# A hybrid recurrent and attention block on one core: gt2's pieces and the DRAM sums placed later, gt2's loads on ScalarE's queue, x1 transposed under the output projection

## The chip, the cores and the metric

The kernel runs on one core of one Trainium2 chip. The metric is the time of one execution on the device in microseconds (us). It was 2109.33 us, the median of three runs (2107.52 to 2113.61). The engines are named as the profile names them: PE (matrix multiplication), PEld (its weight load), DVE (VectorE), ACT (ScalarE), POOL (GpSimd) and SP (the engine that issues most DMAs).

## The reference

One layer on 512 tokens of width 2048, all in 32-bit floats. Six modulation vectors (sh1, sc1, gt1, sh2, sc2, gt2, each of 2048) come from one product of the conditioning vector with a matrix of 2048 x 12288.

```
mod = silu(c) @ w_ada + b_ada;  sh1, sc1, gt1, sh2, sc2, gt2 = split(mod, 6)
h = rms_norm(x, g_mix) * (1 + sc1) + sh1
xr, yr, q, k, v, f_logit = split(h @ w_in)
y_rec = rglru_group(xr, yr, ...)                 # conv, gates, scan, gelu gate
y_att = forgetting_attention_group(q, k, v, f_logit, ...)
mix = concat(rms_norm(y_rec, g_out_rec), rms_norm(y_att, g_out_att))
x = x + gt1 * (mix @ w_out)                      # "x1" in the kernel
h2 = rms_norm(x, g_ffn) * (1 + sc2) + sh2
gate, up = split(h2 @ w_up)                      # width 5632 each
x = x + gt2 * ((silu(gate) * up) @ w_down)
```

## The kernel before, in words

Features lie on the 128 partitions and the 512 tokens along the free dimension, so the width of 2048 is 16 tiles of 128 x 512 (kt 0 to 15). Every product is done in three matmuls of a reduced 32-bit type: weights and activations are each split into a high part (a copy by ACT, line 226) and a low part (a difference by DVE, line 227), and high x high, high x low and low x high are summed in PSUM. So each block of weights passes through SP (load), ACT, DVE and PE. The weights' high and low parts have three buffers each (lines 224 and 225).

The stages of the stretch that matters here:

- The output projection, four groups wo0 to wo3 (line 852). A group makes four tiles of x1 out of 16 steps of 12 matmuls; the function `fm_group` (line 246) calls small functions ("hooks") after given steps. The tiles of a group are read out of PSUM by DVE right behind it; for wo0 to wo2 they are finished (gt1, plus x) by `x1_fin` (line 847) as hooks of the next group, at steps 5, 7, 9 and 11. `square_acc` (line 313) squares each finished tile on ACT and adds it on DVE to the tile ssq_1; `make_hr` (line 836) splits x1 for the up phase.
- The first two up groups, up0 and up1 (line 1000), done in the same way on the unnormalised x1. In up0, hooks at steps 7 and 9 (R1STEP) make r1, the reciprocal root of the mean square: `rstd_parts` (line 284) sums ssq_1 over the partitions with four matmuls, POOL takes the root, four more matmuls spread it over the partitions, and ACT copies it. Hooks at steps 2, 4, 6 and 8 (X_STEPS) run `x1_by_tokens` (line 897): PE transposes a quarter of x1, 16 tiles of 128 x 128 per block, ACT copies it out of PSUM and SP stores it to DRAM, where the end of the kernel reads it. From r1 on, `make_t` (line 913) makes eight sets of sums and differences of the normalised input for the fast phase.
- The fast up phase, f4 to f43 (line 1051). Each f makes its 128 columns with seven products of half size in place of eight; it loads two chunks of 1 MB of weights (`fast_chunk`, line 1020; the loads are line 1029), and makes further sums of blocks on DVE (lines 1038 to 1042).
- The down phases (line 1170), which read sums of weight blocks.

Two kinds of side work run along the up phase. The text places them by n, the number of the chunk (0 to 79):

- gt2: `gt2_piece` (line 174), 64 pieces. A piece is a load of 128 x 512 of the modulation matrix (256 KB, line 171, on SP's queue) and one multiplication on DVE that also sums along the row (line 181). Piece n issues the load of piece n + 1. Its tile has the tag "ssq" with two buffers, which it shares with ssq_x, ssq_att, ssq_rec and ssq_1. The text has piece n at chunk n.
- DRAM sums: `sums24` (line 972), for q from 0 to 10. A sum copies two blocks of 1 MB of the down weights from DRAM to DRAM (lines 975 and 976, on SP, tied behind the last weight load that the text has before it) and then adds three blocks by accumulating DMAs of POOL (line 970). The text begins sum q at chunk 3 + 6q.

The order on each engine's queue is not the order of the text: a planner in the tile framework lays the instructions out by priority (later in the text is lower, `tc.high_priority` raises it) as soon as it believes the inputs and the buffer to be there. Each engine then runs its own list strictly in that order. `ada_some` (line 197) works through the other modulation vectors in the same way, five blocks in each wo group.

Of the kernel before, what the change touches and what calls it, by code (L numbers as in the profile page):

```python
# [39 lines left out]
MIX_STEPS = (12, 13, 14, 15)  # L40
FORGET_STEP = 4
MIXREC_STEPS = (1, 4)
R1STEP = (7, 9)
T_STEPS = ((10, 11, 13, 15), (0, 4, 9, 15))
YR0_AHEAD = 80
CARRY = (0, 0, 1, 1, 1, 3, 3, 6)
# [5 lines left out]
HS = S // 2  # L52
NP = KT // 2
STD = 2
X_STEPS = (2, 4, 6, 8)
NQ = FT // 4


# [5 lines left out]
def block_kernel(ctx, tc, xT, crow, adaT, vecs, bfr, w1, wyr, wqkv0, wqkv, wgate, wout, wup0, wups, wdn, outT):  # L64
# [16 lines left out]
    def page(name, tag, shape=None):  # L81
        return pgp.tile(shape or [P, S], F32, tag=tag, name=name, bufs=TAGS[tag])

    def acc(name):
        return psa.tile([P, S], F32, tag="acc", name=name)
# [82 lines left out]

    def gt2_load(n):
        t = cp.tile([P, S], F32, name=f"gt2_{n}", tag="ssq", bufs=2)  # L170
        nc.sync.dma_start(out=t, in_=adaT[GT2 * KT + n // 4, :, (n % 4) * S:(n % 4 + 1) * S])
        gt2_src[n] = t

    def gt2_piece(n):
# [109 lines left out]
    def rstd_parts(ssq, n, name, inv=None, times=None, bank=None):  # L284

        tok = small(NT, name + "t")
        bank = bank or rgp

        def sums():
            ps = bank(name + "a")  # L290
            for t in range(NT):
                nc.tensor.matmul(ps[:, t:t + 1], lhsT=ssq[:, t * P:(t + 1) * P], rhs=ones[:, 0:1], start=True, stop=True)
            nc.vector.tensor_copy(out=tok, in_=ps[:, :NT])
            rms_rstd(tok, tok, n, inv)
            if times is not None:
                nc.gpsimd.tensor_mul(tok, tok, times)

        def spread():
            pb = bank(name + "b")
            for t in range(NT):  # L300
                nc.tensor.matmul(pb[:, t * P:(t + 1) * P], lhsT=tok[:, t:t + 1].broadcast_to([P, P]), rhs=ident,
                                 start=True, stop=True)
            out = cp.tile([P, S], F32, name=name, tag="rstd_b", bufs=2)
            nc.scalar.activation(out, pb, AF.Copy)
            return out
        return sums, spread
# [6 lines left out]
    def square_acc(ssq, src, first, name, tag):  # L313
        if first:
            nc.scalar.activation(ssq, src, AF.Square)
        else:
            sq = page(name, tag)
            nc.scalar.activation(sq, src, AF.Square)
            nc.vector.tensor_add(ssq, ssq, sq)
# [117 lines left out]
    def add(hooks, n, *fns):  # L437
        hooks.setdefault(n, []).extend(fns)
        return hooks
# [381 lines left out]
    def bank(i, f, name):  # L821
        return acc(name) if i % 2 == 0 else (misc(name) if f < 3 else rgp(name))
# [17 lines left out]
        nc.vector.scalar_tensor_tensor(out=R(l), in0=x1[kt], scalar=s, in1=h, op0=ALU.mult, op1=ALU.subtract)  # L840
        hr.append((h, l))

    ssq_1 = cp.tile([P, S], F32, name="ssq_1", tag="ssq", bufs=2)
    x1 = [None] * KT
    late = []

    def x1_fin(t, kt):
        xt = load_x(kt, "x3_")
        nc.vector.scalar_tensor_tensor(out=t, in0=t, scalar=mods[GT1][:, kt:kt + 1], in1=xt, op0=ALU.mult, op1=ALU.add)
        square_acc(ssq_1, t, kt == 0, f"sq1_{kt}", "d")  # L850

    for g in range(4):
        hk = {}
        for n in range(WO_ADA):
            add(hk, 16 * n // WO_ADA, ada1)
        if g == 0:
            add(hk, MIXREC_STEPS[0], mix_sums)
            add(hk, MIXREC_STEPS[1], mix_rec)
        for n, fn in zip((5, 7, 9, 11), late):
            add(hk, n, fn)  # L860
        late = []
        ps = fm_group(wout[g], korder, mix, f"wo{g}", hooks=hk, ps=[bank(g + 1, f, f"wo{g}p{f}") for f in range(4)])
        for f in range(4):
            kt = g * 4 + f
            t = page(f"x1_{kt}", "c")
            gt = mods[GT1][:, kt:kt + 1]
            if g < 3:
                nc.vector.tensor_mul(t, ps[f], st_att[0])
            else:
                xt = load_x(kt, "x3_")  # L870
                nc.vector.scalar_tensor_tensor(out=t, in0=ps[f], scalar=gt, in1=st_att[0], op0=ALU.mult, op1=ALU.mult)
                nc.vector.tensor_add(t, t, xt)
            x1[kt] = t
            if g < 3:
                late.append(lambda t=t, kt=kt: x1_fin(t, kt))
            else:
                square_acc(ssq_1, t, kt == 0, f"sq1_{kt}", "d")
            if g == 3:
                with_a2()
            if g == 3 and f == 0:  # L880
                for k2 in range(12):
                    make_hr(k2)
            if g == 3:
                make_hr(kt)
    r1 = []
    x1t = {}
    T = {p: [None] * NP for p in range(1, 8)}
    b11 = []
    t_tags = ["b"] * 14 + ["h"] * 28 + ["h"] * 4 + ["b"] * 2 + ["c"] * 8
# [1 line left out]
    def make_h2(kt):  # L891
# [1 line left out]
        nc.vector.scalar_tensor_tensor(out=t, in0=x1[kt], scalar=a2[:, kt:kt + 1], in1=r1[0], op0=ALU.mult, op1=ALU.mult)  # L893
        nc.scalar.activation(t, t, AF.Identity, bias=mods[SH2][:, kt:kt + 1])
        return t

    def x1_by_tokens(a):
        for t in range(NT):
            pt = acc(f"x1p{a}_{t}")
            for k in range(4):  # L900
                nc.tensor.transpose(out=pt[:, k * P:(k + 1) * P], in_=x1[4 * a + k][:, t * P:(t + 1) * P], identity=ident)
            w = page(f"x1w{a}_{t}", "d")
            nc.scalar.activation(w, pt, AF.Copy)
            x1t[t, a] = drp.tile([P, S], F32, name=f"x1t{a}_{t}")
            nc.sync.dma_start(out=x1t[t, a], in_=w)

    def t_split(src, name):
        hi, lo = page(name + "h", t_tags.pop(0)), page(name + "l", t_tags.pop(0))
# [63 lines left out]
    def sums24(q, n):  # L972
        if n == 0:
            with tc.issue_after(up_loads[-1]):
                nc.sync.dma_start(out=s2d[q], in_=wdn[0, q])
                nc.sync.dma_start(out=s4d[q], in_=wdn[1, q])
        elif n < 3:
            dram_sum(s2d[q], wdn[n + 1, q])
        else:
            dram_sum(s4d[q], s2d[q])  # L980
# [19 lines left out]
    for gi in range(STD):  # L1000
        hk = {}
        if gi == 0:
            r1_sums, r1_spread = rstd_parts(ssq_1, D, "rstd_1", bank=acc)
            add(hk, R1STEP[0], r1_sums)
            add(hk, R1STEP[1], lambda: r1.append(r1_spread()))
            for a in range(4):
                add(hk, X_STEPS[a], lambda a=a: x1_by_tokens(a))
        for j in range(4):
            add(hk, T_STEPS[gi][j], lambda j=j + 4 * gi: make_t(j))
        bu_acc = cp.tile([P, S], F32, name=f"bu_acc{gi}", tag="rstd_b", bufs=2)  # L1010
        ps = fm_group(wup0[gi], list(range(KT)), hr, f"up{gi}", hooks=hk, raw_hook=lambda q, raw: up_bias(q, raw, bu_acc),
                      ps=[bank(gi + 1, f, f"up{gi}p{f}") for f in range(4)])
        up_last = up_fin(gi, ps, bu_acc)
        if gi < STD - 1:
            up_last()
# [35 lines left out]
    for f in range(2 * STD, FT):  # L1051
        ps = [bank(f + 1, b, f"uf{f}p{b}") for b in range(4)]
        m = {p: ps[b][:, h * HS:(h + 1) * HS] for p, (b, h) in where.items()}
        for c in range(2):
            for p, hi, lo in fast_chunk(f, c):
                for k in range(4):
                    th, tl = T[p][c * 4 + k]
                    ks = slice(k * P, (k + 1) * P)
                    for n, (w, x) in enumerate(((hi, th), (hi, tl), (lo, th))):
                        first, last = c + k + n == 0, c == 1 and k == 3 and n == 2  # L1060
                        nc.tensor.matmul(m[p], lhsT=R(w[:, ks]), rhs=R(x), start=first and p in opens, stop=last,  # L1061
                                         skip_group_check=True)
            if f == 2 * STD and c == 0:
                up_last()
            n = 2 * (f - 2 * STD) + c
            if n < 4 * KT:
                gt2_piece(n)
            if 3 <= n < 3 + 6 * NQ and n % 6 in (3, 4, 5, 0):
                sums24((n - 3) // 6, (n - 3) % 6)
        g, u = page(f"ug{f}", "c"), page(f"uu{f}", "c")  # L1070
        w1_, w2_ = (ap_.tile([P, S], F32, tag="x", name=f"uw{f}_{i}", bufs=2) for i in range(2))
        two = lambda t: t.rearrange("p (a b) -> p a b", a=2)
        twice = lambda t: t.unsqueeze(1).broadcast_to(halves)
        nc.scalar.activation(w1_[:, lo_half], m[1], AF.Copy)
        nc.vector.tensor_add(two(g), two(ps[0]), twice(w1_[:, lo_half]))
        nc.vector.tensor_sub(two(w2_), twice(g[:, hi_half]), two(ps[1]))
        nc.vector.tensor_add(g[:, hi_half], m[3], w2_[:, lo_half])  # L1077
        nc.vector.tensor_sub(u[:, lo_half], m[4], w2_[:, hi_half])
        nc.vector.tensor_sub(u[:, hi_half], m[5], w2_[:, hi_half])
        nc.scalar.activation(g, g, AF.Silu)  # L1080
        nc.vector.tensor_mul(g, g, u)
        keep_act(g, f)
# [196 lines left out]
```

## Time and profile before

| what | value |
| --- | --- |
| median of 3 runs | 2109.33 us |
| profiled execution | 2112.08 us, span 2110.4 us |
| mean granted PE clock | 0.989 |
| wo2, 16 steps | 646.06 to 689.58 us |
| up0 and up1, with f4 | 733 to 871 us |
| f5 to f14 | 871 to 1097 us |
| f15 to f43 | 1097 to 1681 us |
| gt2 pieces on DVE, 64 | 620.0 to 1074.2 us |

The profile is of one execution. Times are counted from the span's start, and the execution's own time (2112.08 us) is the span and what lies around it. A row of the chain of waits or of a timeline has the start, the length and what ran ("PE wo2p L231 x192": 192 matmuls of line 231 into the tiles wo2p0 to wo2p3). A row of the waits has who waited for whom, the total in us, how often and the longest. The names of tiles appear without their numbers, so that "gt" is gt2_0 to gt2_63, "uq_0sl" is the low part of a sum of the first chunk of any f, and "uf8p" is the PSUM of f8. An instruction of an engine whose name ends in q (SPq) is one of its queue, such as the issue of a DMA.

### The profile page before, as it was taken

The numbers are of one execution on the slowest core, as the hardware profiler recorded it, in microseconds if no ns is written. First come the engines' busy times: TensorE is split into PE (matmuls) and PEld (weight loads), VectorE is DVE, ScalarE is ACT, GpSimd is POOL, SyncE is SP. The second block draws the span as 40 slices with busy tenths as digits, with TensorE's granted clock in tenths as the row PEclk, the third lists the DMA queues.
The fourth block names the chain that finished last, engine by engine and source line by source line (L and its number), as shares of the span: only waits on it lengthen the run. The fifth ranks groups of instructions, "written<-read, shape, count | busy, mean of one in ns | idle before, by whom it ended". The sixth has DMA issues, their size and how long they took to land.

```text
span 2110.4 us, 32392 instructions
## 1 busy us (share of the span) xinstructions
PE 2050.9 (97%) x12537; PEld 1861.0 (88%) x12537; DVE 1719.2 (81%) x2562; ACT 946.9 (45%) x1315; POOL 93.0 (4%) x111
## 2 busy tenths in 40 slices
PE   8999999999999999989899999999999999999999
PEld 6889898898788877989899999999999978888887
DVE  8999768886887579969788888888888877777785
ACT  4433447774532255433344444443444444545543
POOL 0000000100100000000000000000000000000000
PEclk9999999999999999999999999999999999999999
DMA  9989766667678962597698876777743587677794
GB/s 337 353 281 316 253 217 213 226 222 242 238 262 276 269 219 93 162 237 228 198 231 224 235 221 201 208 219 215 198 133 127 181 270 248 240 235 254 247 317 153
DMA packets 168412, 485.21 MB, mean 230 GB/s; under 512 B 20033, under 2 KB 45025, under 8 KB 163810
## 3 DMA queue, kind: packets, MB, share of 16 engines
q1 hardware_dynamic: 158114, 446.44, 62.1%
q0 software_dynamic: 10144, 36.70, 9.7%
q8 instruction: 98, 1.61, 0.3%
q14 instruction: 56, 0.46, 0.1%
HBM read 447.40 MB, written 93.35 MB: 256 GB/s over the span
## 4 chain that ended last, share of the span: by engine, by line
PE 72%; DVE 12%; DMA 10%; issue 3%; ACT 1%; POOL 1%; SPq 1%; DVEq 0%; ACTq 0%
DMA gt<-in_adaT 5%; PE w1p L231 4%; PE dn7p L231 3%; PE dn1p L231 3%; PE dn6p L231 2%; PE yr1p L231 2%; PE wo2p L231 2%; PE wo1p L231 2%; PE dn5p L231 2%; PE yr0p L231 2%; PE wo0p L231 2%; PE dn4p L231 2%; PE up0p L231 2%; PE h2p L231 2%; PE h3p L231 2%
## 5 line engine op out<-in xcount | busy, mean ns | idle before, releaser
L153 DVE SCALAR_TENSOR_TENSOR ada<-ada,c_b 128x1024 f32<-128x1024 f32 x96 | 116.1, 1219 | 29.2 <-DMA ada<-in_adaT 29.0
L226 ACT ACTIVATE uq_0sh<-uq_0r 128x1024 fp32r<-128x1024 f32 x40 | 42.4, 1059 | 140.2 <-DVE uq_0r L1039 134.0
L181 DVE SCALAR_TENSOR_TENSOR gt<-gt,c_b 128x512 f32<-128x512 f32 x64 | 43.8, 687 | 50.4 <-DMA gt<-in_adaT 50.3
L226 ACT ACTIVATE uq_1sh<-uq_1r 128x1024 fp32r<-128x1024 f32 x40 | 42.4, 1060 | 89.2 <-DVE uq_1r L1039 86.2
L227 DVE TENSOR_TENSOR uq_0al<-uq_0r,uq_0ah 128x1024 fp32r<-128x1024 f32 x40 | 48.9, 1224 | 35.8 <-ACT uq_0ah L226 35.8
L227 DVE TENSOR_TENSOR uq_0tl<-uq_0r,uq_0th 128x1024 fp32r<-128x1024 f32 x40 | 48.9, 1223 | 29.7 <-ACT uq_0th L226 29.7
L970 POOL DMA_DIRECT2D s2d<-in_wdn x44 | 36.8, 910 | 743.8 <-DMA s2d<-in_wdn 743.8
L226 ACT ACTIVATE uq_0ah<-uq_0r 128x1024 fp32r<-128x1024 f32 x40 | 42.3, 1058 | 57.8 <-DMA td<-tw 16.4
L226 ACT ACTIVATE uq_1ah<-uq_1r 128x1024 fp32r<-128x1024 f32 x40 | 42.3, 1059 | 46.1 <-issue 44.9
L227 DVE TENSOR_TENSOR uq_0sl<-uq_0r,uq_0sh 128x1024 fp32r<-128x1024 f32 x40 | 49.0, 1225 | 16.3 <-ACT uq_0sh L226 16.3
L226 ACT ACTIVATE uq_0th<-uq_0r 128x1024 fp32r<-128x1024 f32 x40 | 42.3, 1057 | 38.5 <-DVE uq_0r L1042 3.2
L227 DVE TENSOR_TENSOR uq_1tl<-uq_1r,uq_1th 128x1024 fp32r<-128x1024 f32 x40 | 48.9, 1223 | 8.1 <-ACT uq_1th L226 8.1
L226 ACT ACTIVATE uq_1th<-uq_1r 128x1024 fp32r<-128x1024 f32 x40 | 42.3, 1057 | 29.2 <-PE uf17p L1061 1.0
L1080 ACT ACTIVATE ug<-ug 128x512 f32<-128x512 f32 x40 | 25.3, 633 | 63.7 <-DVE ug L1077 63.5
L231 PE MATMUL w1p<-hph,w1h 128*128 128x512 f32 x128 | 47.1, 396 | 6.1 <-ACT hph L372 6.1
L231 PE MATMUL w1p<-hpl,w1h 128*128 128x512 f32 x128 | 50.7, 396 | 0.1
L231 PE MATMUL w1p<-hph,w1l 128*128 128x512 f32 x128 | 50.4, 394 | 0.0
L1038 DVE TENSOR_TENSOR uq_0r<-uq_0r 128x1024 f32<-128x1024 f32 x40 | 48.7, 1218 | 0.0
L227 DVE TENSOR_TENSOR uq_1sl<-uq_1r,uq_1sh 128x1024 fp32r<-128x1024 f32 x40 | 48.7, 1218 | 0.0
L227 DVE TENSOR_TENSOR uq_1al<-uq_1r,uq_1ah 128x1024 fp32r<-128x1024 f32 x40 | 48.6, 1215 | 0.0
L1038 DVE TENSOR_TENSOR uq_1r<-uq_1r 128x1024 f32<-128x1024 f32 x40 | 48.6, 1214 | 0.0
L163 DVE SCALAR_TENSOR_TENSOR ada<-ada,c_b 128x1024 f32<-128x1024 f32 x32 | 39.0, 1217 | 2.6 <-DMA ada<-in_adaT 2.6
(12773 smaller groups left out, 8171.8 us busy)
## 6 DMA issues: line engine op xcount, KB each, us to landing
ada<-in_adaT SPq DMA_DIRECT2D x128, 512.0 KB, 5.1
uq_1r<-in_wups SPq DMA_DIRECT2D x80, 512.0 KB, 4.9
uq_0r<-in_wups SPq DMA_DIRECT2D x80, 512.0 KB, 5.8
s2d<-in_wdn POOLq DMA_DIRECT2D x44, 512.0 KB, 9.2
adf<-in_adaT SPq DMA_DIRECT2D x32, 512.0 KB, 5.9
gt<-in_adaT SPq DMA_DIRECT2D x64, 256.0 KB, 4.2
s4d<-s2d POOLq DMA_DIRECT2D x22, 512.0 KB, 9.0
x<-in_xT SPq DMA_DIRECT2D x32, 256.0 KB, 5.7
```

Of the source, the lines that this page charges most:

```text
L153: nc.vector.scalar_tensor_tensor(out=t, in0=t, scalar=1.0, in1=cs, op0=ALU.mult, op1=ALU.mult, accum_out=ac)
L163: nc.vector.scalar_tensor_tensor(out=t, in0=t, scalar=1.0, in1=c_b[:, cs], op0=ALU.mult, op1=ALU.mult, accum_out=ada_acc[j][:, hf, i:i + 1])
L181: nc.vector.scalar_tensor_tensor(out=t, in0=t, scalar=1.0, in1=c_b[:, r * S:(r + 1) * S], op0=ALU.mult, op1=ALU.mult, accum_out=gt2_acc[:, ...
L226: nc.scalar.activation(R(hi[:, :n]), raw_ap, AF.Copy)
L227: tail_lo.append(nc.vector.tensor_sub(R(lo[:, :n]), raw_ap, hi[:, :n]).ins)
L231: nc.tensor.matmul(ps, lhsT=R(l), rhs=R(r), start=start, stop=stop)
L970: nc.gpsimd.dma_start(out=out[:, cs], in_=src[:, cs], accum_op=ALU.add)
L1038: nc.vector.tensor_add(blocks[:, 0:3:2], blocks[:, 0:2], blocks[:, 2:3].broadcast_to([P, 2, 512]))
L1080: nc.scalar.activation(g, g, AF.Silu)
```

## The change

The first sum of squares is no longer made from x1's own layout. `x1_by_tokens` runs for the tiles of wo0, wo1 and wo2 as a hook at step 13 of the following wo group, in the PSUM banks that the group before used, and only for the tiles of wo3 in up0, at step 6. Each transposed block is copied by ACT as before, with a raised priority, and ACT then squares the copy and sums along the row (`accum_out`), since a row is now a token. The 16 sums go to the tile ss1, and `rstd_parts` adds four of them by one DVE instruction in place of the four matmuls and a copy. R1STEP moves from (7, 9) to (8, 10). ssq_1 and its 16 squares and 15 additions are gone. gt2's loads are issued by ACT. The text has gt2's piece n at chunk n + 16 (GT2_AT) and begins sum q at chunk 14 + 6q (SUMS_AT).

```diff
-R1STEP = (7, 9)
+R1STEP = (8, 10)
...
-X_STEPS = (2, 4, 6, 8)
+X_STEPS = (13, 13, 13, 6)
+GT2_AT, SUMS_AT = 16, 14
...
     def gt2_load(n):
-        nc.sync.dma_start(out=t, in_=adaT[GT2 * KT + n // 4, :, (n % 4) * S:(n % 4 + 1) * S])
+        nc.scalar.dma_start(out=t, in_=adaT[GT2 * KT + n // 4, :, (n % 4) * S:(n % 4 + 1) * S])
...
         def sums():
-            ps = bank(name + "a")
-            for t in range(NT):
-                nc.tensor.matmul(ps[:, t:t + 1], lhsT=ssq[:, t * P:(t + 1) * P], rhs=ones[:, 0:1], start=True, stop=True)
-            nc.vector.tensor_copy(out=tok, in_=ps[:, :NT])
+            if len(ssq.shape) == 3:
+                nc.vector.tensor_reduce(out=tok, in_=ssq, axis=AX.X, op=ALU.add)
+            else:
...
-    ssq_1 = cp.tile([P, S], F32, name="ssq_1", tag="ssq", bufs=2)
+    ss1 = cp.tile([P, NT, 4], F32, name="ss1")
...
+    def x1_by_tokens(a):
+        for t in range(NT):
+            pt = bank(a + 1, t, f"x1p{a}_{t}")
+            for k in range(4):
+                nc.tensor.transpose(out=pt[:, k * P:(k + 1) * P], in_=x1[4 * a + k][:, t * P:(t + 1) * P], identity=ident)
+            w, sq = page(f"x1w{a}_{t}", "d"), page(f"x1s{a}_{t}", "d")
+            with tc.high_priority(offset=EVAC):
+                nc.scalar.activation(w, pt, AF.Copy)
+            nc.scalar.activation(sq, w, AF.Square, accum_out=ss1[:, t, a:a + 1])
+            x1t[t, a] = drp.tile([P, S], F32, name=f"x1t{a}_{t}")
+            nc.sync.dma_start(out=x1t[t, a], in_=w)
...
-        square_acc(ssq_1, t, kt == 0, f"sq1_{kt}", "d")
...
+        if g:
+            add(hk, X_STEPS[g - 1], lambda a=g - 1: x1_by_tokens(a))
...
-            else:
-                square_acc(ssq_1, t, kt == 0, f"sq1_{kt}", "d")
...
-            r1_sums, r1_spread = rstd_parts(ssq_1, D, "rstd_1", bank=acc)
+            r1_sums, r1_spread = rstd_parts(ss1, D, "rstd_1", bank=acc)
...
-            for a in range(4):
-                add(hk, X_STEPS[a], lambda a=a: x1_by_tokens(a))
+            add(hk, X_STEPS[3], lambda: x1_by_tokens(3))
...
-            if n < 4 * KT:
-                gt2_piece(n)
-            if 3 <= n < 3 + 6 * NQ and n % 6 in (3, 4, 5, 0):
-                sums24((n - 3) // 6, (n - 3) % 6)
+            if 0 <= n - GT2_AT < 4 * KT:
+                gt2_piece(n - GT2_AT)
+            if 0 <= n - SUMS_AT < 6 * NQ and (n - SUMS_AT) % 6 < 4:
+                sums24((n - SUMS_AT) // 6, (n - SUMS_AT) % 6)
```

The old `x1_by_tokens` (lines 897 to 905) is the new one without the square, with the banks of the "acc" pool.

More of the change, by code (lines that the diff above doesn't have):

```diff
@@ L289, in sums @@
         def sums():
-            ps = bank(name + "a")
-            for t in range(NT):
-                nc.tensor.matmul(ps[:, t:t + 1], lhsT=ssq[:, t * P:(t + 1) * P], rhs=ones[:, 0:1], start=True, stop=True)
-            nc.vector.tensor_copy(out=tok, in_=ps[:, :NT])
+            if len(ssq.shape) == 3:
+                nc.vector.tensor_reduce(out=tok, in_=ssq, axis=AX.X, op=ALU.add)
+            else:
+                ps = bank(name + "a")
+                for t in range(NT):
+                    nc.tensor.matmul(ps[:, t:t + 1], lhsT=ssq[:, t * P:(t + 1) * P], rhs=ones[:, 0:1], start=True, stop=True)
+                nc.vector.tensor_copy(out=tok, in_=ps[:, :NT])
             rms_rstd(tok, tok, n, inv)
@@ L841, in make_hr @@
         hr.append((h, l))
-    ssq_1 = cp.tile([P, S], F32, name="ssq_1", tag="ssq", bufs=2)
+    ss1 = cp.tile([P, NT, 4], F32, name="ss1")
     x1 = [None] * KT
+    x1t = {}
+    def x1_by_tokens(a):
+        for t in range(NT):
+            pt = bank(a + 1, t, f"x1p{a}_{t}")
[7 more added lines that the diff above has]
+            nc.sync.dma_start(out=x1t[t, a], in_=w)
     late = []
@@ L885, in block_kernel @@
     r1 = []
-    x1t = {}
     T = {p: [None] * NP for p in range(1, 8)}
@@ L895, in make_h2 @@
         return t
[L897 to L905, printed above, removed]
     def t_split(src, name):
```

## The prediction

> **What bounds the kernel now.** I read the page first, then the stretches (busy time of each engine by stage), then the waits of PE, DVE and SP, and the chain for the lengths of the stages.
>
> ```profile
> span 2110.4 us, 32392 instructions
> ...
> PE 2050.9 (97%) x12537; PEld 1861.0 (88%) x12537; DVE 1719.2 (81%) x2562; ACT 946.9 (45%) x1315; POOL 93.0 (4%) x111
> ```
>
> PE is the bound, so what counts is where PE stands still or is late. The stretches: wo1 to wo3; the first up group until r1 is there; from there to the last split for f4; f5 to f14; the rest of the up phase. Columns: from and to, length, then busy time of PE, PEld, DVE, ACT and POOL with counts, granted clock, DMA share, GB/s.
>
> ```profile
> 602.50:733.10 130.60, 130.60 (x578) 108.18 (x577) 94.56 (x147) 39.98 (x49) 5.22 (x6) 1.00 0.86 283
> 733.10:777.40 44.30, 39.59 (x202) 33.11 (x201) 30.50 (x50) 18.93 (x30) 2.14 (x2) 0.92 0.71 236
> 777.40:868.50 91.10, 82.91 (x433) 71.81 (x431) 87.83 (x158) 49.94 (x74) 0.00 (x0) 0.96 0.34 114
> 868.50:1096.80 228.30, 212.49 (x1701) 210.74 (x1700) 191.39 (x298) 81.54 (x101) 14.90 (x18) 0.96 0.77 211
> 1096.80:1681.00 584.20, 584.20 (x4871) 584.20 (x4870) 490.07 (x637) 246.09 (x293) 34.65 (x42) 1.00 0.68 198
> ```
>
> The first and the last run at a full PE. Between them PE stands still, and its clock drops to 0.92 and 0.96 besides. Who makes it wait there is in the waits of PE from 733 to 1097 (total us, times, longest), and how much is lost comes from the chain (start, length, what):
>
> ```profile
> PE uf8p L1061 <- DVE uq_0sl L227: 6.3, 1, 6.3
> PE bup_p L995 <- DVE bu_acc L940: 5.1, 1, 5.1
> PE x1p L901 <- DVE x L871: 4.7, 2, 4.3
> PE uf11p L1061 <- DVE uq_0tl L227: 4.7, 1, 4.7
> ```
>
> ```profile
> 646.06 43.52 PE wo2p L231 x192
> 689.58 16.11 PE wo3p L231 x71
> ```
>
> ```profile
> 756.68 1.75 PE x1p L901 x16
> ```
>
> ```profile
> 871.17 19.68 PE uf5p L1061 x164
> ...
> 1096.83 20.16 PE uf15p L1061 x168
> ```
>
> A group of 16 steps takes 43.52 us of PE, a step 2.72, so wo3 ends at 689.58 + 43.52 = 733.10. From there to 871.17, the start of f5, are 138.07. The work in them is two groups (87.04), four blocks of transposes (7.00) and f4 (20.16), together 114.2, with the few small matmuls of sums and biases not counted. **Loss one is at most 23.9 us.** f5 to f14 took 1096.83 - 871.17 = 225.66 for ten of 20.16. **Loss two is 24.1 us.** Nearly all these waits name DVE, so the waits of DVE (870 to 1100) and of SP (whole span) come next:
>
> ```profile
> DVE gt L181 <- DMA gt<-in_adaT: 32.3, 13, 6.6
> ```
>
> ```profile
> SPq L171 <- DVE gt L181: 117.0, 43, 11.3
> ```
>
> The first is behind loss two: DVE sits 32.3 us before gt2 pieces that have not landed, and the splits queued behind them come late to PE. When do they not land? The SP queue shows where a DRAM sum (L975) starts; below it are stretches of four such bursts, with one gap (the second row).
>
> ```profile
> 906.69 0.76 SPq L975 DMA_DIRECT2D s2d<-in_wdn  x1
> ...
> 927.25 15.74 SPq L171 DMA_DIRECT2D gt<-in_adaT  x4
> 943.79 0.98 SPq L1029 DMA_DIRECT2D uq_0r<-in_wups  x2
> ...
> 969.01 0.80 SPq L1029 DMA_DIRECT2D uq_0r<-in_wups  x2
> ```
>
> ```profile
> 906.00:948.00 42.00, 35.65 (x276) 35.45 (x275) 26.05 (x40) 12.16 (x15) 5.04 (x6) 0.88 0.99 248
> 948.00:979.00 31.00, 30.37 (x246) 29.68 (x246) 29.70 (x49) 11.97 (x15) 0.00 (x0) 1.00 0.53 176
> 979.00:1016.00 37.00, 32.30 (x265) 32.10 (x264) 28.88 (x45) 11.84 (x15) 4.90 (x6) 0.96 1.01 279
> 1052.00:1087.00 35.00, 33.34 (x276) 32.93 (x275) 29.52 (x47) 12.46 (x16) 4.97 (x6) 1.00 1.01 241
> 1110.00:1145.00 35.00, 35.00 (x294) 35.00 (x293) 29.87 (x40) 14.47 (x18) 4.93 (x6) 1.00 0.97 268
> ```
>
> PE loses in the bursts, little in the gap. The burst at 1110 is as dense (DMA share 0.97) and PE loses nothing in it. The difference is that the gt2 pieces were over by then. DVE's time on the piece's line alone, two records a piece:
>
> ```profile
> 573.00:733.00 160.00, 9.75 (x28) 1.00 0.83 273
> 733.00:871.00 138.00, 11.12 (x32) 0.95 0.46 155
> 871.00:969.00 98.00, 11.06 (x32) 0.95 0.73 208
> 969.00:1097.00 128.00, 12.37 (x36) 0.96 0.81 214
> ```
>
> So 14 pieces ran under the output projection, 16 up to f4, 34 beside f5 to f14 (18 of them after 969), none later, although the program's text puts piece 0 at f4 and the last at f35. The order on the engines is not the text's: a piece fills DVE as soon as its buffer is free.
>
> **The change part by part.** *The buffer.* The pieces share the two "ssq" buffers, and ssq_1 holds one of them until r1's sums. The change has no ssq_1 (the squares go to the small ss1), so the pieces have two places from the first mix sums on.
>
> ```profile
> L171 SPq DMA_DIRECT2D gt<-in_adaT x64: 327/328/1087, 609.9 to 1069.4; - x64
> ```
>
> ```profile
> gt<-in_adaT SPq DMA_DIRECT2D x64, 256.0 KB, 4.2
> ```
>
> ```profile
> L181 DVE SCALAR_TENSOR_TENSOR gt<-gt,c_b 128x512 f32<-128x512 f32 x8 | 5.5, 684 | 0.0
> ```
>
> With one place a piece costs its issue (0.33), its landing (4.2) and its work (0.68) one after the other; with two, the next load is under way meanwhile. I take it that the 14 under the output projection become about 28.
>
> *The places in the text.* GT2_AT moves the pieces 16 chunks later. Since they ran far ahead of their place, I expect little of that; they still start early. SUMS_AT is different: a sum is tied to the last weight load that the text has before it, so sum q moves from f(5 + 3q), second chunk, to f(11 + 3q), first chunk. Sum 1 stands at 906.69, behind f8's second load; five loads on, at 969.01, is f11's first. So sum 0 starts near 969 by this trace's clock, and sooner as the losses before it go. By 969 the trace had 46 of the 64 pieces done. With 14 more done under the output projection some 60 are, when the first burst comes. The last sum moves to f41, still ahead of the down phases that read it: no cost.
>
> So loss two goes but for the last few pieces. I take back 20 of the 24.1; the ends are 0 and 24.
>
> *r1 and loss one.* r1's spread ended here:
>
> ```profile
> L301 PE MATMUL rstd_1b<-ident,rstd_1t x8: 271/275/275, 776.4 to 777.2; 128*128 128x128 f32 x8
> ```
>
> In the change three blocks (5.25 us of PE) stand under wo1 to wo3, so up0 begins at 738.35. Only x1's last block is in it, at step 6, and the spread follows step 10: 738.35 + 11 x 2.72 + 1.75 = 770.0, 7 us sooner although a step later. The 4.7 us for which a block waited for wo3's evacuation go, as the block at step 6 finds it done. What is late next is DVE: from r1 to f4's last split it was busy 87.83 of 91.10 us, 5.5 of it with eight pieces. Without pieces and idle time that is 82.3, and f4's last split is at 852.3 instead of 868.5, 16.2 sooner; with both kept it is at 861.1, 7.4 sooner. PE's own floor for the end of f4, 738.35 + 87.04 + 1.75 + 20.16 = 847.3, is earlier still. I take 14, near the first, since most pieces are earlier; the ends are 7 and 20.
>
> *The squares.* Fifteen adds leave DVE; as many squares stay on ACT:
>
> ```profile
> L319 DVE TENSOR_TENSOR ssq<-ssq,sq x15: 677/683/693, 610.8 to 751.9; 128x512 f32<-128x512 f32 x15
> ```
>
> Eleven or twelve of them lie under wo1 to wo3, 8 us, and make room there for 14 more pieces (9.5 us). DVE was idle there for 130.60 - 94.56 = 36 us, so this is hidden. The new sum over four columns touches 16 elements a partition; nothing.
>
> *The transposes' place.* They take the banks of the group before, read out at this group's start; x1 of that group is finished from steps 5 to 11, and PE asks at 13. Four stores a block go on SP behind the copies, and weight and modulation loads queue behind them. For this and the extra piece loads I take 2 us, with ends of 0 and 6; DVE's idle time is the cover.
>
> *The queue.* 64 issues of 0.33 us move to ACT, 21 us on an engine 45% busy: hidden. SP is rid of its waits for the pieces' places: the row at 927.25 held it for 15.74 us, and the next weights were issued right behind, at 943.79. That gain is within loss two.
>
> Here the Trainium skill speaks against the change. "DMA: Bandwidth & Descriptors", section "Issuing engines are not separate DMA queues", says that transfers issued by different engines share the same DMA engines and interleave, and only issue time is saved. By that rule the new queue lets no piece land sooner in a burst, and the first rival's time holds if the meetings stay; the trace of before has no load on ACT's queue to show it.
>
> *Sum:* -20 - 14 + 2 = -32 us. The profiled execution took 2112.08 (span 2110.4), so 2080.1; it lies 2.75 above the median of the runs, and from the median it is 2109.33 - 32 = **2077**.
>
> **The rivals.** *Bursts and pieces meet again (0.12).* If the pieces are no earlier than now, sums 0 and 1 meet the last 18. Loss two stays whole, and -14 + 2 gives 2097. For: a second place helps only where DVE has time. Against: its 36 idle us.
>
> *The pieces run where the text puts them (0.08),* f12 to f43, and each of eleven bursts meets some. The burst at 1052, where DVE had got somewhat ahead, did 276 matmuls where the one at 1110 did 294 in the same 35 us: 18 x 0.12 = 2.2 us. Eleven make 24 and eat loss two: 2109.33 - 24 - 14 + 2 + 24 = 2097 again. Against: all 64 ran early in this trace.
>
> *ACT is held, slower (0.15).* A load waits for the place that an earlier piece frees; on SP these waits were 117.0 us in 43, 2.7 each. On ACT the copies of the next weights (L226) stand behind it, DVE's differences behind those, and PE behind them. If 24 pieces fall after 770, where DVE has no time to spare, and each wait passes on whole, this costs 65, less the 32 won: 2142. It decides from 32 / 24 = 1.3 us a piece. Against: ACT is idle half the time, and a chunk's copies are 10.1 us of PE ahead.
>
> *No net change (0.08).* Other late work takes DVE's time and PE wins nothing: 2109.
>
> **How the numbers follow.** The forecast has 0.57, with a range of its own of 2066 to 2090 (24 and 19 won, or 12 and 9, about). Faster by over 0.3% (6 us, about what a measurement of this kernel can tell from no change): 0.57 + 0.12 + 0.08 = 0.77; within it 0.08; slower 0.15. The range of 2064 to 2107 leaves out the slower rival and half of the unchanged one.
>
> **What would show it.** Right: pieces begin before 600 and are nearly over when the first sum bursts; wo1 to wo3 take some 45.3 us each; r1's spread ends near 770; f5 starts near 856; every f from f5 on takes 20.2. Wrong: DVE waits of tens of us for gt; DVE or PE waiting for ACT behind a held load; a wo group of over 48; many pieces left after the first burst.

## The result and the profile after

The kernel after takes 2126.36 us (median of five runs, 2122.55 to 2128.89), the kernel before on the same chip 2112.07 (2107.52 to 2117.20). The ratio is 1.0068, with a 95% interval of 1.0045 to 1.0090: **slower by 0.7%**, where 2077 was forecast. From the page of after:

```profile
span 2120.8 us, 32408 instructions
...
PE 2054.4 (97%) x12529; PEld 1860.5 (88%) x12529; DVE 1712.2 (81%) x2547; ACT 951.7 (45%) x1331; POOL 92.3 (4%) x111
```

DVE has 7 us less to do than before, as meant, and the span is longer. The stretches of after: wo1 to wo3; until r1's spread ends; until f4 ends (the row of before stopped 2.7 us short of that, at f4's last split); f5 to just behind f14.

```profile
602.70:767.70 165.00, 145.89 (x625) 117.65 (x623) 108.54 (x206) 42.01 (x59) 0.00 (x0) 0.92 0.76 262
767.70:811.90 44.20, 35.97 (x157) 29.23 (x158) 30.97 (x56) 19.42 (x35) 1.20 (x2) 0.93 0.63 180
811.90:905.00 93.10, 87.48 (x440) 75.00 (x439) 85.78 (x144) 50.13 (x73) 0.00 (x0) 0.93 0.33 93
905.00:1108.00 203.00, 203.00 (x1694) 203.00 (x1693) 171.77 (x225) 86.49 (x103) 10.18 (x12) 1.00 0.62 182
```

The last row is loss two, and it is gone: PE is full, and f5 to f14 take 201.4 us by their first and last matmuls where they took 225.7. The loss sits in the first row, where before had none: 165.0 us in place of 130.6. Of these 34.4, the three moved blocks are 5.25; PE stands still for 165.00 - 145.89 = 19.1; and the rest, 145.89 - 130.60 - 5.25 = 10.0, is work done at a granted clock of 0.92 in place of 1.00. The two rows between, which hold loss one, sum to 137.3 (before, up to f4's end: 138.1). Of PE's waits from 600 to 1100 in after the three longest are these:

```profile
PE wo2p L232 <- ACT x1w L858: 9.2, 3, 3.9
PE wo3p L232 <- ACT x1w L858: 9.1, 2, 6.8
PE rstd_1b L305 <- POOL rstd_1t L281: 4.5, 1, 4.5
```

A wo group cannot begin since its banks still hold the transposes that ACT has not copied. (In after the piece is L182, its load L172, the high copy L227, the low part L228, the matmul L232, the copy of a block L858.) Why ACT is late, and why DVE is, from the waits in the same stretch:

```profile
ACT wo_1h L227 <- DVE gt L182: 48.4, 9, 10.1
ACT wo_0h L227 <- DVE gt L182: 15.6, 3, 6.4
```

```profile
DVE gt L182 <- DMA gt<-in_adaT: 46.5, 17, 7.5
```

DVE stands 46.5 us before pieces that have not landed, and ACT 64 us before loads whose place DVE has not freed. The timeline of ACT in after shows how it stands: "ACTq L172" are the loads it issues, and the brackets give the idle time before an instruction.

```profile
634.95 0.95 ACTq L172 DMA_DIRECT2D gt<-in_adaT  x2
636.00 1.06 ACT L227 ACTIVATE wo_1h<-wo1r 128x1024 fp32r<-128x1024 f32 x1 [7.65 <-DVE gt L182]
639.60 8.75 ACTq L172 DMA_DIRECT2D gt<-in_adaT  x4
648.45 1.06 ACT L227 ACTIVATE wo_0h<-wo2r 128x1024 fp32r<-128x1024 f32 x1 [11.39 <-PE wo1p L232]
```

From this I formed a first theory, *the queue*: ScalarE computes behind loads that wait for a place. Two rivals: *the places* (two buffers let so many pieces under the output projection that they crowd DVE, whoever loads) and *the blocks* (x1's transposes and their banks hold the wo groups).

### The profile page after: what moved, and what is told of

It is laid out like the page before. It is cut to its first block, busy times and chain, and to the rows that moved or that the text cites. A ratio compares the mean times of both kernels' runs of the same rounds, so it can differ in the third digit from the quotient of the medians.

```text
span 2120.8 us, 32408 instructions
## 1 busy us (share of the span) xinstructions
PE 2054.4 (97%) x12529; PEld 1860.5 (88%) x12529; DVE 1712.2 (81%) x2547; ACT 951.7 (45%) x1331; POOL 92.3 (4%) x111
## 4 chain that ended last, share of the span: by engine, by line
PE 71%; DVE 13%; DMA 11%; issue 3%; ACT 1%; POOL 1%; SPq 0%; DVEq 0%; ACTq 0%
PE w1p L232 4%; DMA gt<-in_adaT 3%; PE dn7p L232 3%; PE dn1p L232 3%; PE dn5p L232 2%; PE dn6p L232 2%; PE yr1p L232 2%; PE dn4p L232 2%; PE yr0p L232 2%; PE h3p L232 2%; PE h2p L232 2%; PE h7p L232 2%; PE dn3p L232 2%; DVE ada L154 1%; PE dn2p L232 1%
## 5 line engine op out<-in xcount | busy, mean ns | idle before, releaser
L227 ACT ACTIVATE uq_0sh<-uq_0r 128x1024 fp32r<-128x1024 f32 x40 | 42.4, 1060 | 110.8 <-DVE uq_0r L1043 110.8
L227 ACT ACTIVATE uq_1sh<-uq_1r 128x1024 fp32r<-128x1024 f32 x40 | 42.4, 1061 | 107.9 <-DVE uq_1r L1043 107.9
L228 DVE TENSOR_TENSOR uq_0al<-uq_0r,uq_0ah 128x1024 fp32r<-128x1024 f32 x40 | 49.0, 1224 | 47.3 <-ACT uq_0ah L227 45.2
L182 DVE SCALAR_TENSOR_TENSOR gt<-gt,c_b 128x512 f32<-128x512 f32 x64 | 43.0, 686 | 48.6 <-DMA gt<-in_adaT 48.3
L228 DVE TENSOR_TENSOR uq_0tl<-uq_0r,uq_0th 128x1024 fp32r<-128x1024 f32 x40 | 49.0, 1224 | 39.7 <-ACT uq_0th L227 39.7
L227 ACT ACTIVATE uq_0ah<-uq_0r 128x1024 fp32r<-128x1024 f32 x40 | 42.4, 1059 | 69.3 <-DMA td<-tw 14.5
L227 ACT ACTIVATE uq_1ah<-uq_1r 128x1024 fp32r<-128x1024 f32 x40 | 42.4, 1061 | 57.0 <-issue 57.0
L227 ACT ACTIVATE uq_0th<-uq_0r 128x1024 fp32r<-128x1024 f32 x40 | 42.4, 1060 | 48.0 <-DVE uq_0r L1046 2.1
L228 DVE TENSOR_TENSOR uq_0sl<-uq_0r,uq_0sh 128x1024 fp32r<-128x1024 f32 x40 | 49.0, 1225 | 18.1 <-ACT uq_0sh L227 18.1
L227 ACT ACTIVATE uq_1th<-uq_1r 128x1024 fp32r<-128x1024 f32 x40 | 42.4, 1060 | 37.0 <-PE uf25p L1065 1.0
L228 DVE TENSOR_TENSOR uq_1tl<-uq_1r,uq_1th 128x1024 fp32r<-128x1024 f32 x40 | 49.0, 1224 | 10.9 <-ACT uq_1th L227 10.9
L232 PE MATMUL w1p<-hph,w1h 128*128 128x512 f32 x128 | 47.3, 398 | 4.9 <-ACT hph L376 4.9
L232 PE MATMUL w1p<-hpl,w1h 128*128 128x512 f32 x128 | 50.9, 398 | 0.0
L232 PE MATMUL w1p<-hph,w1l 128*128 128x512 f32 x128 | 50.7, 396 | 0.0
L228 DVE TENSOR_TENSOR uq_1sl<-uq_1r,uq_1sh 128x1024 fp32r<-128x1024 f32 x40 | 48.6, 1215 | 0.0
L228 DVE TENSOR_TENSOR uq_1al<-uq_1r,uq_1ah 128x1024 fp32r<-128x1024 f32 x40 | 48.6, 1214 | 0.0
L164 DVE SCALAR_TENSOR_TENSOR adf<-adf,c_b 128x1024 f32<-128x1024 f32 x32 | 39.0, 1219 | 0.1
```

The costliest lines, as they stand in the source:

```text
L164: nc.vector.scalar_tensor_tensor(out=t, in0=t, scalar=1.0, in1=c_b[:, cs], op0=ALU.mult, op1=ALU.mult, accum_out=ada_acc[j][:, hf, i:i + 1])
L182: nc.vector.scalar_tensor_tensor(out=t, in0=t, scalar=1.0, in1=c_b[:, r * S:(r + 1) * S], op0=ALU.mult, op1=ALU.mult, accum_out=gt2_acc[:, ...
L227: nc.scalar.activation(R(hi[:, :n]), raw_ap, AF.Copy)
L228: tail_lo.append(nc.vector.tensor_sub(R(lo[:, :n]), raw_ap, hi[:, :n]).ins)
L232: nc.tensor.matmul(ps, lhsT=R(l), rhs=R(r), start=start, stop=stop)
```

## The experiments

All times are medians; ratios are to the kernel before in alternating runs on the same chip. The first four kernels met a before of 2114.47, the next four of 2111.68, the last four of 2114.01. Each group ran on a chip of its own, so kernels of different groups are compared by their ratios and by the stages of their traces.

**The loads back on SyncE, the rest as after.**

```diff
-        nc.scalar.dma_start(out=t, in_=adaT[GT2 * KT + n // 4, :, (n % 4) * S:(n % 4 + 1) * S])
+        nc.sync.dma_start(out=t, in_=adaT[GT2 * KT + n // 4, :, (n % 4) * S:(n % 4 + 1) * S])
```

> The changed kernel with gt2's loads back on SP. Theory A (the queue: ACT is held by the loads that wait for a place, and the copies of weights and x1 behind them come late): wo1 to wo3, which took 165 us with their gaps from 602.7 to 767.7, fall to some 140, and the kernel takes about 2095 to 2100. Theory B (the places: with two buffers the pieces crowd into the output projection, their landings are slow there and DVE stands before them): wo1 to wo3 stay above 155, the kernel at 2115 to 2126. Theory C (the blocks: the next group waits for the banks of x1's blocks, whoever loads gt2): wo1 to wo3 stay at 160, the kernel at 2120.

2092.99 us, ratio 0.9889 (0.9868 to 0.9909): this one line is worth 33 us by the medians, 38 by the ratios. Two places and the blocks under the output projection are both still there, so neither rival explains the loss by itself.

**The kernel before, with the loads on ScalarE alone** (the same line, the other way).

> The kernel before with gt2's loads on ACT's queue and nothing else. Theory A: ACT is held in wo1 to wo3 here too, though by fewer loads; the stage grows from 130.5 us by 5 to 15, the kernel to 2117 to 2127. Theories B and C: the stage stays within 2 us, the kernel at 2112.

2141.45, ratio 1.0118 (1.0100 to 1.0136): 27 us slower. wo1 to wo3 take 160.6 us in place of 130.7. The waits there:

```profile
DVE gt L181 <- DMA gt<-in_adaT: 50.4, 10, 10.5
ACT wo_0h L226 <- DVE gt L181: 46.1, 5, 19.5
ACT wo_1h L226 <- DVE gt L181: 28.5, 6, 6.6
```

The same loop with a single place, at 20 pieces there, without any block under the projection.

**The kernel before, with the pieces and the sums later alone.**

```diff
+GT2_AT, SUMS_AT = 16, 14
...
-            if n < 4 * KT:
-                gt2_piece(n)
-            if 3 <= n < 3 + 6 * NQ and n % 6 in (3, 4, 5, 0):
-                sums24((n - 3) // 6, (n - 3) % 6)
+            if 0 <= n - GT2_AT < 4 * KT:
+                gt2_piece(n - GT2_AT)
+            if 0 <= n - SUMS_AT < 6 * NQ and (n - SUMS_AT) % 6 < 4:
+                sums24((n - SUMS_AT) // 6, (n - SUMS_AT) % 6)
```

> The kernel before with GT2_AT = 16 and SUMS_AT = 14 alone (pieces and sums later in the text, loads on SP, x1 and r1 as before). All theories: loss two (f5 to f14, 225.7 us instead of 201.6) shrinks by 15 to 24 as the bursts no longer meet the pieces; loss one is as before or up to 5 better since sum 0 leaves wo3; 2090 to 2097. If instead the shift in the text only moves the meetings, the kernel stays at 2112.

2090.52, ratio 0.9884 (0.9864 to 0.9904). Two constants do all that the whole change does with its loads on SyncE.

**The kernel before, with x1's part alone** (the blocks, the squares by tokens, R1STEP and X_STEPS).

> The kernel before with x1's part alone (blocks under wo1 to wo3, squares by tokens, no ssq_1, R1STEP 8 and 10); pieces and sums at their places in the text of before, loads on SP. Theory A: wo1 to wo3 at about 136 (130.5 and the 5.25 of the blocks), r1 somewhat sooner, 2095 to 2112. Theory B: the pieces crowd, wo1 to wo3 above 150. Theory C: wo1 to wo3 above 150 with PE waiting for ACT's copies of x1. B and C: 2120 or more.

2110.94, ratio 0.9980 (0.9964 to 0.9995): 3.5 us. With the run with SyncE, 2.5 us *above* the two constants alone, x1's part is worth about nothing. By the traces it wins 15.4 us in f5 to f14, where fewer pieces are left for the bursts, and gives back 6.2 in wo1 to wo3 and 5.5 from there to f4's end.

**The loads on GpSimd**, to hold nobody who computes.

```diff
-        nc.scalar.dma_start(out=t, in_=adaT[GT2 * KT + n // 4, :, (n % 4) * S:(n % 4 + 1) * S])
+        nc.gpsimd.dma_start(out=t, in_=adaT[GT2 * KT + n // 4, :, (n % 4) * S:(n % 4 + 1) * S])
```

> The kernel after with one line changed: the 64 loads of gt2 are issued by GpSimd. The queue theory says that ScalarE lost the time because it computes behind the loads that it issues; GpSimd has next to nothing to compute under the output projection, so the loads may stand there: about 2093 us (2088 to 2098), as with the loads on SyncE, and no wait of ScalarE for a piece on VectorE. The rival says that loads that leave SyncE's order overtake the weights there and come in the wrong places whoever issues them: then about 2126, as the kernel after (2118 to 2130). Between: GpSimd raises r1's sums to the power, behind loads that wait for a place; if it holds r1, r1's spread ends some us after the 780.9 of the run with SyncE, and the time follows by as many: 2095 to 2102.

2124.24, ratio 1.0049 (1.0034 to 1.0065): as slow as after, and **the theory of the held ScalarE falls**. Its waits from 602 to 775, which is from 5 us ahead of wo1 to the end of wo3:

```profile
POOL gt L172 <- DVE gt L182: 139.2, 45, 7.3
DVE gt L182 <- DMA gt<-in_adaT: 50.9, 27, 4.4
ACT x1w L858 <- DMA x1t<-x1w: 28.2, 3, 13.2
```

GpSimd waits for the places, ScalarE for no piece; DVE stands before pieces as long as in after (50.9 against 46.5). PE's own waits there are 14.1 us for the copies of blocks and 8.8 for low parts of weights. (I read the last row as a consequence: SP waits 75.6 us for DVE's late "ada" products, and x1's stores queue behind those loads. No run tests this reading.) So I read DVE's own order. The timeline of DVE with the loads on GpSimd, and under it that with the loads on SyncE, late in wo1:

```profile
649.50 0.69 DVE L182 SCALAR_TENSOR_TENSOR gt<-gt,c_b 128x512 f32<-128x512 f32 x1 [4.40 <-DMA gt<-in_adaT]
...
650.14 0.69 DVE L182 SCALAR_TENSOR_TENSOR gt<-gt,c_b 128x512 f32<-128x512 f32 x1
...
653.75 0.69 DVE L182 SCALAR_TENSOR_TENSOR gt<-gt,c_b 128x512 f32<-128x512 f32 x1 [2.91 <-DMA gt<-in_adaT]
...
654.37 1.22 DVE L228 TENSOR_TENSOR wo_0l<-wo2r,wo_0h 128x1024 fp32r<-128x1024 f32 x1
```

```profile
640.61 0.69 DVE L182 SCALAR_TENSOR_TENSOR gt<-gt,c_b 128x512 f32<-128x512 f32 x1 [1.86 <-DMA gt<-in_adaT]
...
641.25 0.69 DVE L182 SCALAR_TENSOR_TENSOR gt<-gt,c_b 128x512 f32<-128x512 f32 x1
...
641.87 1.22 DVE L228 TENSOR_TENSOR wo_0l<-wo2r,wo_0h 128x1024 fp32r<-128x1024 f32 x1
```

Three pieces in a row, with two places: the third's load cannot start before the first piece is done, and the weights' low part stands behind the third. On SyncE two stand in a row, and other work follows. Counted from the timelines of DVE between the start of wo1 and the end of wo3, with the idle time ahead of the pieces there:

| kernel | places | pieces there | rows of two | rows of three or four | DVE before pieces, us |
| --- | --- | --- | --- | --- | --- |
| before | 1 | 14 | 0 | 0 | 12.8 |
| before, loads on ScalarE | 1 | 20 | 2 | 0 | 50.4 |
| after, loads on SyncE | 2 | 31 | 8 | 0 | 13.9 |
| after (ScalarE) | 2 | 49 | 7 | 7 | 46.7 |
| after, loads on GpSimd | 2 | 50 | 9 | 5 | 48.8 |

In the three kernels with two places, no row is longer than the places on SyncE; on another queue the pieces come thicker and some rows are longer. This order is fixed when the kernel is built. The new theory, *the order*: the planner lays the pieces down more densely when their loads leave SyncE, and DVE then stands for landings with the weights behind it.

How much of the standing do the long rows hold? By the place of a piece in its row, 27.5 of the 46.7 us in after lie before the third of a row. With GpSimd it is 14.8 of 48.8 before the third or fourth, and 34.1 before the first and second. In before with ScalarE it is 13.7 of 50.4 before the second of a row, and the rest before pieces that stand first or alone. So the long rows explain more than half in after, under a third in the other two; for the rest the number of pieces, or the time at which their loads are issued, may count. No run separates these.

**The later sums without the later pieces**: the third kernel with GT2_AT at 0, the places of before, and SUMS_AT at 14.

> The kernel before with SUMS_AT at 14 alone; the pieces keep their step from the start of the up phase. If the gain of the later sums is all that SUMS_AT and GT2_AT give together, and the pieces' text place does little because their loads and the scheduler place them, this gives the 2090.5 of the run with both (2087 to 2095). The rival, that the pieces must be moved too, since those of the first up steps crowd VectorE before f4: r1's stages last as before and the gain is about half, 2100 (2097 to 2106).

2088.70, ratio 0.9886 (0.9861 to 0.9912). The sums alone are the gain; the place of the pieces in the text is worth nothing that these runs can tell, as the prediction had it.

**The pages of the squares, and r1 sooner**, with the loads on SyncE.

```diff
-R1STEP = (8, 10)
+R1STEP = (7, 8)
-X_STEPS = (13, 13, 13, 6)
+X_STEPS = (13, 13, 13, 5)
-            w, sq = page(f"x1w{a}_{t}", "d"), page(f"x1s{a}_{t}", "d")
+            w = page(f"x1w{a}_{t}", "d")
-            nc.scalar.activation(sq, w, AF.Square, accum_out=ss1[:, t, a:a + 1])
+            nc.scalar.activation(pt, w, AF.Square, accum_out=ss1[:, t, a:a + 1])
```

> The kernel after with the loads on SyncE, and then: the squares are written over the bank of the transposes in place of a second page, x1's last blocks stand at step 5, r1's sums and spread at 7 and 8 in place of 8 and 10. In the run with SyncE the last square waited 7.3 us for a page of which the store to DRAM had not landed, and r1's spread ended at 780.9, 37.3 us behind the start of up0. If r1 sets loss one and the pages set r1, the spread ends at about 770 and the time falls by as much as r1: 2093 less 11, about 2082 (2078 to 2088). The rival says that loss one is set by the work that follows r1 (VectorE's splits and products for h2) whenever it starts, or that the banks held by the squares cost the groups as much: r1 sooner, the time 2090 to 2095.

2088.26, ratio 0.9881 (0.9864 to 0.9897). r1 came as expected, the time did not: by the ratios it is 1.7 us below the run with SyncE, inside the intervals, in place of 11. The rows of the copy of r1, with SyncE and then with this kernel (the two starts behind the durations):

```profile
L308 ACT ACTIVATE rstd<-rstd_1b x1: 599/599/599, 780.9 to 780.9; 128x512 f32<-128x512 f32 x1
```

```profile
L308 ACT ACTIVATE rstd<-rstd_1b x1: 599/599/599, 770.1 to 770.1; 128x512 f32<-128x512 f32 x1
```

**r1 sooner in the kernel with the two constants.**

```diff
-R1STEP = (7, 9)
+R1STEP = (5, 7)
```

> The kernel before with GT2_AT 16 and SUMS_AT 14, and r1's sums and spread at steps 5 and 7 in place of 7 and 9; squares and transposes as before. In the run with the two constants alone the last square was added at 748.0 and the sums were computed only at 763.7, the spread ended at 771.9. If loss one follows r1 one for one, the spread ends at about 765 and the time is 2090.5 less 7, about 2084 (2080 to 2088). The rival, that r1 is ready when it is needed and something else sets loss one: 2088 to 2093.

2085.79, ratio 0.9870 (0.9854 to 0.9886): the lowest of the complete versions ("the fastest" below), though its interval overlaps with those of the four others under 2093. Counted from the end of wo3 its r1 is 7.2 us sooner than with the two constants alone and f4 ends 0.8 us *later*. So what it may have gained on that kernel (3 us by the ratios, inside the intervals) does not come from there: of the 5.2 between the two profiled spans 2.7 lie ahead of wo1 already, where the two do the same. What r1 runs into is in these two stretches of this kernel, from r1 to just behind up1, and from there into f5 (the third busy time is DVE's):

```profile
762.00:833.00 71.00, 68.34 (x313) 56.28 (x311) 64.88 (x123) 38.64 (x60) 0.00 (x0) 1.00 0.41 140
833.00:868.00 35.00, 29.73 (x209) 28.80 (x210) 32.20 (x50) 16.72 (x23) 0.00 (x0) 0.85 0.41 133
```

Up to the end of up1 PE is busy 68.34 of 71.00 us, so an earlier r1 has next to nothing left to win there. The loss lies behind it, before f4's work: PE is busy 29.73 of 35.00 us at a clock of 0.85, DVE 32.20.

**No piece under the output projection, the loads on ScalarE.** Two idle tiles take both places until wo3's first result.

```diff
+    hold = [cp.tile([P, S], F32, name=f"hold{i}", tag="ssq", bufs=2) for i in range(2)]
+    for t in hold:
+        nc.vector.memset(t[:, :1], 0.0)
...
             if g == 3 and f == 0:
+                for h_ in hold:
+                    nc.vector.tensor_copy(h_[:, :1], t[:, :1])
```

> The kernel after, loads of gt2 on ScalarE, with gt2's two places taken by two idle tiles until wo3's first result is there: no piece can run under the output projection. The run with the loads on GpSimd lost the time without holding ScalarE, so a new theory, the order: with the loads on a queue of their own the scheduler writes three pieces in a row into VectorE's order (on SyncE two at most); the third's load starts when the first has freed its place, and VectorE stands for a landing with the weights' low halves behind it. It says that wo1 to wo3 take 45.5 us each again, and that what is lost comes with rows of pieces in the up stages: 2105 (2096 to 2113). The rival, that ScalarE's or any second queue disturbs the weights' own loads by itself, has wo1 to wo3 slow with no piece there: over 2115.

2102.84, ratio 0.9959 (0.9940 to 0.9978): some 23 us below after, with ScalarE's queue kept. **The same with the loads on SyncE:**

> As the run before it, with the loads on SyncE. The order's theory: wo1 to wo3 45.5 each; all 64 pieces stand after 745, some of them then in the first DRAM sums (two or three us each at f10 and f11): 2097 (2091 to 2104), and less than the run with ScalarE's queue by what the rows of three cost in the up stages. The rival, that the queue costs the same wherever the pieces stand, puts some 30 us between the two.

2105.74, ratio 0.9965 (0.9949 to 0.9981). The queue that was worth 33 us is worth nothing that can be told once no piece runs under the output projection. The rows of the pieces' line in wo1 to wo3, up to f4, and f5 to f14, and the first stretch whole, all of the kernel with ScalarE:

```profile
603.62:739.67 136.05, 0.00 (x0) 1.00 0.67 231
739.67:867.10 127.43, 12.52 (x36) 0.97 0.41 143
867.10:1106.70 239.60, 31.85 (x92) 0.98 0.74 221
```

```profile
603.62:739.67 136.05, 136.05 (x626) 113.40 (x625) 84.25 (x115) 48.58 (x73) 0.00 (x0) 1.00 0.67 231
```

PE is full in the first. In the last, 46 pieces run beside the sums, and f5 to f14 take 219.4 us: part of loss two is back.

**Later sums still**: the fastest version with SUMS_AT at 19. Steps 1 to 3 of the last sum then have no chunk left and are left out, six of 66 accumulating transfers, so the down phase reads unfinished blocks there.

> The fastest version so far (sums later, r1 at steps 5 and 7, loads on SyncE, squares and blocks as before) with SUMS_AT at 19 in place of 14. In its trace the last pieces ran to 1008, the first sums' burst to 990, and f10 took 25.7 us, f11 21.1, the others 20.3. If the burst met the last pieces there, later sums give both back: 2085.8 less 6, about 2080 (2077 to 2084). The rival, that the burst disturbs the weights of the up phase themselves whenever it comes: one stage stays 25 us long some 50 us later, the time 2084 to 2088.

2082.01, ratio 0.9861 (0.9837 to 0.9886). Chains from 960 on: the fastest version (a landing in its first burst), then this one.

```profile
964.83 9.40 DMA gt<-in_adaT
```

```profile
965.65 20.16 PE uf10p L1062 x168
985.82 20.16 PE uf11p L1062 x168
```

In the first, f10 and f11 take 46.7 us by their matmuls, and a piece in the burst takes 9.4 us to land; in the second the pieces are over at 1000.6, and the sums' first burst, which starts at 1002.7, finds none. There f5 to f14 take 201.1 us with 29 pieces beside them, as long as in after with none: pieces without bursts cost nothing there, and bursts without pieces cost nothing either. Loss two is their meeting. (The six transfers left out did not make it faster: from the end of f43 on it takes 428.7 us, the fastest version 427.6.)

**The kernel after without 62 of the 64 loads**; the products stay.

```diff
+        if n >= 2:
+            gt2_src[n] = gt2_first[n % 2]
+            return
...
-        nc.vector.scalar_tensor_tensor(out=t, in0=t, scalar=1.0, in1=c_b[:, r * S:(r + 1) * S], op0=ALU.mult, op1=ALU.mult,
+        nc.vector.scalar_tensor_tensor(out=t, in0=c_b[:, r * S:(r + 1) * S], scalar=1.0, in1=c_b[:, r * S:(r + 1) * S], op0=ALU.mult, op1=ALU.mult,
```

> The kernel after, of which 62 of gt2's 64 loads are left out: each piece multiplies the condition with itself, so gt2 is not what the reference asks for; the 64 products on VectorE stay. The order's theory says that VectorE lost its time standing for loads: without them wo1 to wo3 take 45.5 us each and the time is 2085 (2070 to 2095). The rival, that the moved blocks with their copies and banks, or the products' own time on VectorE, delay the groups: wo2 and wo3 stay over 50 us, the time over 2105.

2081.91, ratio 0.9862 (0.9838 to 0.9886). The stretch of wo1 to wo3, whole and the pieces' line alone:

```profile
607.09:743.50 136.41, 136.35 (x626) 113.29 (x625) 116.16 (x232) 48.13 (x73) 0.00 (x0) 1.00 0.66 222
```

```profile
607.09:743.50 136.41, 37.20 (x116) 1.00 0.66 222
```

58 products run there, nine more than in after, some of them seven in a row, and PE is full. So the products' time and their rows cost nothing by themselves; the loads do. The run takes out at once DVE's standing for them, ACT's standing behind their issue, and their traffic.

## Why the prediction was wrong

Lengths of the stages, in us, from the first and last matmuls of each kernel's trace:

| kernel | wo1 to wo3 | r1 spread behind wo3 | wo3's end to f4's end | f5 to f14 |
| --- | --- | --- | --- | --- |
| before | 130.7 | 44.3 | 138.1 | 225.7 |
| after | 165.0 | 44.2 | 137.4 | 201.4 |
| before, loads on ScalarE | 160.6 | 43.4 | 141.2 | 219.3 |
| after, loads on SyncE | 136.5 | 37.1 | 133.1 | 201.1 |
| after, loads on GpSimd | 167.1 | 42.2 | 133.6 | 201.4 |
| the two constants alone | 130.7 | 36.1 | 130.8 | 208.4 |
| the sums later alone | 130.7 | 36.1 | 131.3 | 208.8 |
| x1's part alone | 136.9 | 47.6 | 143.6 | 210.3 |
| squares over the bank, r1 sooner (SyncE) | 136.1 | 28.2 | 130.2 | 201.1 |
| two constants, r1 sooner | 130.7 | 28.9 | 131.6 | 207.2 |
| the same, sums later still | 130.7 | 28.9 | 128.0 | 201.1 |
| no piece under wo, ScalarE | 136.1 | 34.3 | 127.5 | 219.4 |
| no piece under wo, SyncE | 136.1 | 32.6 | 127.2 | 219.8 |
| after, no loads | 136.4 | 33.6 | 121.9 | 201.4 |

f15 to f43 take 584.6 in all of them. After against before: +34.3 - 0.7 - 24.3, and 1.2 elsewhere, make the 10.5 us between the two profiled executions.

*Loss two, right.* Forecast 20 of 24.1, got 24.3. The mechanism was the one named: the sums come when the pieces are over (in after the last piece ran at 800.9, the first sum began at 988.6). This is no gift of the failed step: with SyncE the last piece ran at 930.5 and the first sum began at 960.1.

*The step that failed: "The queue. 64 issues of 0.33 us move to ACT ... hidden"*, with the buffer's step that 28 pieces under the output projection fit into DVE's idle time. Both priced work, and the work was indeed hidden (58 products cost nothing). Neither priced the landings that DVE stands for. The queue was put at nothing and cost 33 us. With the loads off SyncE, 49 pieces came under wo1 to wo3, some in rows longer than the two places, and the chain of after from 620 to 720 says what that costs:

```profile
by line: DMA gt<-in_adaT 38.7%; DMA ada<-in_adaT 10.5%; DVE ada L154 10.2%; DVE gt L182 9.2%; issue 7.6%; DMA x<-in_xT 6.9%; DMA wo2r<-in_wout 6.6%; DMA x1t<-x1w 5.2%; DVE wo_0l L228 4.5%; DVE wo_1l L228 2.5%; DVE x L886 1.8%; DVE hrl L844 
```

The prediction had written that the order on the engines is not the text's; it then took that order as given while it changed what the order is made from. The same sentence of the Trainium skill ("DMA: Bandwidth & Descriptors", "Issuing engines are not separate DMA queues") held in this: the median landing is 4.6 us in after and was 4.2, so the new queue let no load land faster.

*The slower rival, right in sign.* "ACT is held" forecast 2142, with pieces after 770 that pass on their waits. ACT was held, 64 us, but before 770 (10 pieces only ran between wo3's end and f4's), and GpSimd's run shows that the time goes without ACT being held. In the kernel before with ScalarE's loads the rows do not exceed the one place but twice, and there ACT's own standing behind the loads, 74.6 us, may be the larger part; that was not separated.

*Loss one, forecast 14, got nothing.* Two steps fail. First, r1: forecast 31.7 us behind wo3's end, with SyncE 37.1, since the last square there waits 7.3 us for a page that a store to DRAM still holds; squares and copies share four "d" pages, which the prediction did not look at. Second, and more: r1 does not move f4 one for one. Brought forward by 8.9 us (squares over the bank) and by 7.2 (two constants), it moved f4's end by -2.9 and +0.8. Part of what r1 won DVE then stood away before pieces that had not landed: from wo3's end to f4's end 8.6 us in place of 3.0, and 8.3 in place of 3.6. Where the sums come later still, with r1 as early, this standing is 3.9 us and f4 ends 3.6 us sooner. DVE's work and its standing behind r1 are what is left to set f4; without a piece there and without a landing the stretch took 121.9 us, in the run without loads. No run tests DVE's work by itself. The prediction had the 82.3 us of it in its hand and still let r1's start move all of it.

What did win time in loss one, the prediction put at nothing. In before sum 0 starts under wo3, and its accumulating transfers are issued until 729.9:

```profile
701.12 0.63 SPq L975 DMA_DIRECT2D s2d<-in_wdn  x1
```

With SUMS_AT alone it starts at 955.4. From wo3's end until r1's spread PE then has no wait and a clock of 1.00 (before: 39.59 us busy of 44.30, at 0.92), and f4's end comes 6.8 us sooner behind wo3's. The kernel with x1's part alone begins sum 0 at 711.3, after with SyncE at 960.1, and the same stretch is 10.5 us shorter in the second. So SUMS_AT pays in both losses.

*Right besides*: a wo group of 45.3 us with a block (45.45 to 45.9 with SyncE), the squares hidden (with SyncE PE is busy 136.35 of the 136.50 us of wo1 to wo3), and GT2_AT without effect.

*Open*: why the planner packs the pieces more densely when their loads leave SyncE was not tried, nor was after's queue with SyncE's order. That the loss needs both a queue other than SyncE's and pieces under the output projection is shown by the runs; that the order on DVE carries it is read from the timelines.

## What to carry to other kernels

Moving a load to another queue can change the order that is written for the engines that use it, and that may weigh more than the issue time saved: compare the orders of the two builds, count the small users that moved, and look for rows of them longer than their buffers. Here idle time of DVE hid 58 products, but not the landings that the weights' low parts stood behind. Where a change has several parts, try the cheapest alone: here two constants, one of them idle, gave 24 us.

## What was not expected of the hardware

The granted clock of PE fell with its standing: 0.92 over the 165 us of wo1 to wo3 in after, 1.00 in the same stage with SyncE. Beside 19.1 us of standing, the matmuls took 10.0 us more. The two other kernels that stand in this stage agree: 20.3 us of standing and 9.7 more of matmuls in before with ScalarE, 22.9 and 8.3 with GpSimd, both at 0.94. A piece that lands in 4.2 to 4.6 us at the median took 9.4 in a burst of DRAM sums.
